# RWKV-7 recurrence in a decoder trunk: decay applied after the state's addition, norms folded, gate applied last

## The chip, the cores and the metric

One core of one Trainium2 chip runs the whole program. The metric is device time in microseconds (us); a kernel is run several times and the median counts. The engines of the core are named as in the profile: PE (TensorE, matrix products), PEld (its weight loads), DVE (VectorE), ACT (ScalarE), POOL (GpSimd) and SP (SyncE, which issues the transfers). Each engine works through its own instructions in a fixed order and waits on semaphores for the others.

## What is computed

Two decoder layers for one sequence of 256 tokens of width 2048, in fp32: an RWKV-7 time mixing layer and a differential attention layer, each followed by a gated MLP. The change touches only the time mixing. Its core, per head of 64:

```python
kk = kk / jnp.maximum(jnp.sqrt(jnp.sum(kk * kk, -1, keepdims=True)), 1e-12)
k = k * (1 + (a - 1) * k_a)
decay = jnp.exp(-jnp.exp(w.astype(jnp.float32)))
# S_t = S_{t-1} (diag(w_t) + a_t^T b_t) + v_t^T k_t ;  y_t = S_t r_t
y = wkv7_scan(r_h, decay, k_h, v_h, -kk, kk * a_h)
mean = y.mean(-1, keepdims=True)
var = jnp.square(y - mean).mean(-1, keepdims=True)
y = ((y - mean) * lax.rsqrt(var + GN_EPS)).reshape(B, T, D) * lnx_g + lnx_b
bonus = jnp.sum(r_h * k_h * r_k, -1, keepdims=True) * v_h
return ((y + bonus) * g) @ w_o
```

## The kernel before

Every dense product takes fp32 weights, which come from memory in blocks of 128x512 (`raw`), are rounded by ACT to a high part (`hi`, L217), and split by DVE into a rest (`lo`, L220); PE then does three products with them (L230 to L235). So each block needs one ACT and one DVE instruction ahead of PE. There are 4 raw blocks, 5 of `hi` and 5 of `lo` in the recurrence's stage.

The recurrence is cut into 8 groups of four heads (`NG`), each of 256 tokens in 4 chunks of 64 (`NC`). `pipeline` (L1039) runs stages of different groups side by side: while `chain` and `outputs` work on group i, `lanes` works on i+1, `factors`, `corners` and `bonus` on i+2, and `products`, the dense products for k and r, on i+3. `_together` interleaves their steps by fixed paces (the table `PACE`). The framework then puts the instructions of each engine into one order; what a row waits for goes by semaphores. `issue_after` pins some products of PE behind others.

What the stages do, with the lines that matter:

- `factors` (L1116): the squared norm of k·k_k by a product with block ones (L1138), its lower bound (L1139), the sums of the log decay within a chunk (`L`, a scan, L1146), the same sums without the token's own term (`Lx`, L1148), the inverse square root of the norm (`rsqrt`, L307: logarithm, exponential, one Newton step in three DVE instructions, L313 to L315), three exponentials (L1152 to L1154), the last column of each chunk's decay (`pc`, L1155, on POOL). From these come `KB` (keys divided by the decay so far, L1170 and L1171) and `AR` (minus the unit keys times the decay before the token, L1172; r times the decay up to it, L1174). L1184 forms their products, L1187 masks them into `M`.
- `corners` (L1225): `KB` times `pc` (L1240), eight transposes into `KBT` (L1247), and a small triangular inverse on DVE (L1251 and L1253).
- `lanes` (L1264): the rest of the triangular inverse, 32x32 products.
- `chain` (L1355): per chunk, products into `b0` and `b1` (L1386, L1399), copied to `R` by ACT and DVE; a product (L1413) copied to `UV` by ACT and DVE; the product of `UV` and `KBT` (L1426) that adds to the state `S` (copy at the first chunk, L1433; decay and addition later, L1430); the outputs into `yps` (L1403, L1437). The fourth chunk updates no state.
- `outputs` (L1443): the gate's small product (`lora`), y times gain and gate (L1455), sums of squares (L1459) into the bank `us`, their scaling (L1461), the inverse square root, and the sum with the gated bonus (L1466).
- `gates` (L1343): the small products for decay and a, with weights `l2` cast at L854, and their sigmoids (L1351), which need another function table on ACT than the rest (ACT_TABLE_LOAD at L1351 and L186).

The helper `copy` records at L1090 for every engine. Banks named `pss` are two, shared by `factors`, `corners`, `bonus` and `lanes`; `psd` holds the dense products.

Of the kernel before, what the change touches and what calls it, by code (L numbers as in the profile page):

```python
# [980 lines left out]
def _fl(t):  # L981
    return t.rearrange("p j t -> p (j t)")


# [4 lines left out]
class Groups:
# [126 lines left out]
    def factors(self, g):  # L1116
# [22 lines left out]
        nc.vector.tensor_scalar(out=_fl(t1), in0=ps, scalar1=1e-24, scalar2=None, op0=ALU.max)  # L1139
# [3 lines left out]
        Lx = g1.tile([P, GT, T], F32, name="Lx")  # L1143
        eL = g1.tile([P, GT, T], F32, name="eL")
# [9 lines left out]
        nc.scalar.activation(out=Lx, in_=Lx, func=AF.Exp, scale=-KAPPA)  # L1154
        nc.gpsimd.tensor_copy(out=pc.rearrange("p j c o -> p (j c) o"), in_=_ch(_fl(eL))[:, :, C - 1:C])  # L1155
# [7 lines left out]
        nc.vector.tensor_tensor(out=a, in0=kk, in1=a, op=ALU.mult)  # L1163
# [4 lines left out]
        for par in range(2):  # L1168
# [3 lines left out]
        nc.vector.scalar_tensor_tensor(out=AR[:, :, 0, :], in0=c3, scalar=-1.0, in1=_ch(_fl(Lx)), op0=ALU.mult,  # L1172
                                       op1=ALU.mult)
        nc.vector.tensor_tensor(out=AR[:, :, 1, :], in0=_ch(_fl(r)), in1=_ch(_fl(eL)), op=ALU.mult)  # L1174
# [50 lines left out]
    def corners(self, g):  # L1225
# [3 lines left out]
        d1, d2, KB, pc = s["d1"], self.d2, s["KB"], s["pc"]  # L1229
# [10 lines left out]
        nc.vector.tensor_tensor(out=KB.rearrange("p c a s -> p c (a s)"), in0=KB.rearrange("p c a s -> p c (a s)"),  # L1240
                                in1=pc.rearrange("p j c o -> p (j c) o").broadcast_to([P, GT * NC, 2 * C]),
                                op=ALU.mult)
        yield
# [111 lines left out]
    def chain(self, g):  # L1355
# [36 lines left out]
        for c in range(NC):  # L1392
# [30 lines left out]
            if c < NC - 1:  # L1423
                for jj in range(GT):
                    for h in range(2):
                        mm = nc.tensor.matmul(sp[rows[h], jj, :], lhsT=KBT[:, jj * NC + c, h * 64:h * 64 + 64],  # L1426
                                              rhs=UV[:, jj, c, h, :], start=True, stop=True)
                if c:
                    for jj in range(GT):
                        nc.vector.scalar_tensor_tensor(out=Sn[:, jj, :], in0=S[:, jj, :], scalar=pc[:, jj, c, :],  # L1430
                                                       in1=sp[:, jj, :], op0=ALU.mult, op1=ALU.add)
                else:
                    nc.vector.tensor_copy(out=Sn, in_=sp)  # L1433
# [9 lines left out]
    def outputs(self, g):  # L1443
# [8 lines left out]
        yield from t.lora(self.lp, self.mids, g, 2, lambda ps: self.copy(PACE["eg"], _fl(rs), ps))  # L1452
        nc.scalar.activation(out=y2, in_=yps, func=AF.Square)
        for jj in range(GT):
            nc.vector.scalar_tensor_tensor(out=y[:, jj, :], in0=yps[:, jj, :], scalar=t.p("lnx_g", j0 + jj),  # L1455
                                           in1=rs[:, jj, :], op0=ALU.mult, op1=ALU.mult)
# [85 lines left out]
```

## Time and profile before

| | us |
|---|---|
| median of three runs | 2493.4 |
| lowest, highest | 2493.0, 2501.9 |
| the profiled execution, as timed | 2495.5 |
| its span in the trace | 2493.2 |

The profile's rows are of that one execution. The recurrence's groups take from about 140 to about 580 us of the span; ahead of them lie the token shift and the products for v and the small products, behind them the output product, the attention and the MLPs. How to read the rows: a busy time says how long an engine worked; a wait is the idle time of an engine just before an instruction, put down to the instruction that ended last of those that it needed. In rows of the timeline the first number is the start, the second the duration, and brackets hold the idle time before it. "x16" counts instructions.

### The profile page before, as it was taken

Reading aid. Unit: us, or ns where it says so; the run is one execution under the profiler, and the core shown is the slowest. Engines: PE = TensorE matmul, PEld = TensorE weight load, DVE = VectorE, ACT = ScalarE, POOL = GpSimd, SP = SyncE. Lnnn points to the kernel's source line nnn. Section 1 sums busy time; section 2 is a strip of 40 time slices with the busy share of each in tenths; the row PEclk is TensorE's granted clock in tenths of the full one; section 3 lists DMA queues with packets and bytes.
Section 4 is the critical chain, followed back from the end, with each engine's and each line's share of the span. In section 5 each row is a group of like instructions: output and inputs, shape, how many; then the busy total and the mean of one; then the engine's idle time right before and its main releaser. Section 6 shows DMA issues by size and latency. Waiting matters only on the chain.

```text
span 2493.2 us, 53177 instructions
## 1 busy us (share of the span) xinstructions
PE 2430.3 (97%) x18618; PEld 2160.0 (87%) x18618; DVE 1902.1 (76%) x4282; ACT 1497.6 (60%) x3415; POOL 155.1 (6%) x200
## 2 busy tenths in 40 slices
PE   8999999998999999999999999999999999999997
PEld 7988888777988888888889999988988888888886
DVE  8978888878987777776666866778987777776665
ACT  7755565546766666665555766666766666655554
POOL 0020000002100000001111000003100000001111
PEclk9999999999999999999999999999999999999999
DMA  7644443444566666667665555556566666666663
GB/s 242 192 125 114 116 108 100 115 128 148 162 200 190 190 189 189 190 190 226 189 187 162 174 173 167 175 174 184 167 197 188 187 188 187 189 187 186 190 188 122
DMA packets 276717, 428.49 MB, mean 172 GB/s; under 512 B 60632, under 2 KB 83168, under 8 KB 276448
## 3 DMA queue, kind: packets, MB, share of 16 engines
q1 hardware_dynamic: 276448, 425.10, 58.9%
q8 instruction: 145, 2.38, 0.4%
q14 instruction: 124, 1.02, 0.1%
HBM read 420.25 MB, written 6.31 MB: 171 GB/s over the span
## 4 chain that ended last, share of the span: by engine, by line
PE 82%; DVE 10%; DMA 3%; issue 2%; ACT 2%; SPq 0%; POOL 0%; ACTq 0%; DVEq 0%; POOLq 0%
PE psd L234 43%; PE psd L235 22%; DVE lo L220 3%; PE psd L230 2%; PE psd L232 2%; PE psd L231 2%; DMA raw<-in_rkv 2%; PE psd L283 1%; PE psd L285 1%; PE psd L284 1%; ACT hi L217 1%; PE lnst L339 1%; PE psd L926 1%; PE psd L925 0%; PE psd L927 0%
## 5 line engine op out<-in xcount | busy, mean ns | idle before, releaser
L217 ACT CAST hi<-raw 128x256 fp32r<-128x256 f32 (+3 forms) x2236 | 1078.1, 489 | 805.3 <-PE psd L234 555.9
L220 DVE TENSOR_TENSOR lo<-raw,hi 128x256 fp32r<-128x256 f32 (+3 forms) x2236 | 1148.6, 539 | 483.5 <-ACT hi L217 379.3
L234 PE MATMUL psd<-S,hi 128*128 128x512 f32 x2976 | 1044.1, 395 | 1.2 <-ACT hi L217 0.7
L235 PE MATMUL psd<-S,lo 128*128 128x256 f32 x2976 | 833.5, 280 | 0.5 <-DVE lo L220 0.4
L234 PEld LDWEIGHTS psd<-S,hi 128*128 128x128 f32 x2976 | 559.6, 188 | 131.2 <-ACT hi L217 1.8
L235 PEld LDWEIGHTS psd<-S,lo 128*128 128x128 f32 x2976 | 559.2, 188 | 2.0 <-DVE lo L220 1.9
L234 PE MATMUL psd<-hs,hi 128*128 128x512 f32 x1290 | 451.5, 394 | 0.0
L235 PE MATMUL psd<-hs,lo 128*128 128x256 f32 x1290 | 361.0, 280 | 0.0
L234 PEld LDWEIGHTS psd<-hs,hi 128*128 128x128 f32 x1290 | 241.8, 187 | 56.2 <-ACT hi L217 0.6
L235 PEld LDWEIGHTS psd<-hs,lo 128*128 128x128 f32 x1290 | 243.1, 188 | 0.1
L230 PE MATMUL psd<-S,hi 128*128 128x256 f32 x512 | 149.9, 293 | 9.0 <-ACT hi L217 9.0
L232 PE MATMUL psd<-S,lo 128*128 128x256 f32 x512 | 147.3, 288 | 3.7 <-DVE lo L220 3.6
L231 PE MATMUL psd<-S,hi 128*128 128x256 f32 x512 | 145.5, 284 | 0.0
L234 PE MATMUL psd<-S1r,hi 128*128 128x512 f32 x276 | 106.8, 419 | 3.3 <-ACT hi L217 2.0
L230 PEld LDWEIGHTS psd<-S,hi 128*128 128x128 f32 x512 | 98.1, 192 | 13.0 <-ACT hi L217 9.0
L232 PEld LDWEIGHTS psd<-S,lo 128*128 128x128 f32 x512 | 98.0, 191 | 6.4 <-DVE lo L220 5.2
L231 PEld LDWEIGHTS psd<-S,hi 128*128 128x128 f32 x512 | 98.3, 192 | 0.7 <-issue 0.6
L230 PE MATMUL psd<-S1r,hi 128*128 128x256 f32 x284 | 85.5, 301 | 0.0
L539 DVE SCALAR_TENSOR_TENSOR gc<-gp,cpar,gc 128x256 f32<-128x256 f32 x172 | 82.9, 482 | 2.6
L234 PE MATMUL psd<-S1a,hi 128*128 128x512 f32 x240 | 84.4, 395 | 0.0
L232 PE MATMUL psd<-S1r,lo 128*128 128x256 f32 x284 | 80.8, 284 | 0.3 <-DVE lo L220 0.3
L231 PE MATMUL psd<-S1r,hi 128*128 128x256 f32 x284 | 81.0, 285 | 0.0
(298 smaller groups left out, 3414.7 us busy)
## 6 DMA issues: line engine op xcount, KB each, us to landing
raw<-in_ff_up SPq DMA_DIRECT2D x676, 256.0 KB, 3.7
raw<-in_ff_down SPq DMA_DIRECT2D x320, 256.0 KB, 2.9
raw<-in_rkv SPq DMA_DIRECT2D x192, 256.0 KB, 3.8
raw<-in_da_qk SPq DMA_DIRECT2D x122, 256.0 KB, 3.6
raw<-in_da_v SPq DMA_DIRECT2D x64, 256.0 KB, 3.2
raw<-in_da_o SPq DMA_DIRECT2D x64, 256.0 KB, 3.8
raw<-in_rw_o SPq DMA_DIRECT2D x50, 256.0 KB, 3.5
raw<-in_ff_down SPq DMA_DIRECT2D x32, 192.0 KB, 2.4
```

Of the source, the lines that this page charges most:

```text
L217: nc.scalar.copy(out=hi[:, :s * P], in_=r)
L220: eng.tensor_tensor(out=lo[:, :s * P], in0=r, in1=hi[:, :s * P].bitcast(F32), op=ALU.subtract)
L230: nc.tensor.matmul(ps[:, :T], lhsT=hi, rhs=xs[:, :T], start=first, stop=False)
L231: nc.tensor.matmul(ps[:, :T], lhsT=hi, rhs=xs[:, T:], start=False, stop=False)
L232: nc.tensor.matmul(ps[:, :T], lhsT=lo, rhs=xs[:, :T], start=False, stop=last)
L234: nc.tensor.matmul(ps, lhsT=hi, rhs=xs, start=first, stop=False)
L235: nc.tensor.matmul(ps[:, T:], lhsT=lo, rhs=xs[:, :T], start=False, stop=last)
L283: nc.tensor.matmul(o, lhsT=xh, rhs=hi, start=k == 0 and b == 0, stop=False)
L284: nc.tensor.matmul(o, lhsT=xh, rhs=lo, start=False, stop=False)
L285: nc.tensor.matmul(o, lhsT=xl, rhs=hi, start=False, stop=k == KT - 1 and b == T // P - 1)
L339: self.nc.tensor.matmul(st, lhsT=self.c("onesd"), rhs=t, start=not self.ln_open and n == 0, stop=stop and n == 1)
L539: nc.vector.scalar_tensor_tensor(out=gc, in0=g[:, k:k + T], scalar=cw(k, j), in1=gc, op0=ALU.mult, op1=ALU.add)
```

## The change

- The decay of a chunk (`pc`) is no longer multiplied into `KB`. In its place the updated state is multiplied: S becomes (S + update) times `pc`, in two instructions over both tiles of the group (L1437 and L1438 of the changed kernel), and one at the first chunk.
- The exponentials of the decay go into a tile `eL` with a column of ones ahead of each chunk. The decay before a token is then the same tile read one column back, so `Lx` and its exponential go. The exponentials no longer wait for the inverse square root, which used `eL` as scratch.
- The minus sign moves from `AR` to the product of the unit keys and a.
- A new function `rsqrt_neg` gives minus the inverse square root: ACT squares the first estimate with the scale folded in, and DVE does the Newton step in two instructions. It reads its input with scale and addition folded in, so the outputs' scaling goes, and it may read PSUM. The lower bound of the keys' norm becomes a Relu on ACT.
- In `outputs`, ACT multiplies y by the gain, the gate is kept in the tile `Lx`, and gate times (bonus minus y) comes last, since y carries the minus sign. The sums of squares go to a `pss` bank, held until the Newton step has read it.

```diff
+    def rsqrt_neg(self, v, e, l, scale, bias, add):
+        nc.scalar.activation(out=l, in_=v, func=AF.Ln, scale=scale, bias=bias)
+        nc.scalar.activation(out=e, in_=l, func=AF.Exp, scale=-0.5)
+        nc.scalar.activation(out=l, in_=e, func=AF.Square, scale=math.sqrt(0.5 * scale))
+        nc.vector.scalar_tensor_tensor(out=l, in0=v, scalar=add, in1=l, op0=ALU.add, op1=ALU.mult)
+        nc.vector.scalar_tensor_tensor(out=e, in0=l, scalar=-1.5, in1=e, op0=ALU.add, op1=ALU.mult)
...
-        nc.vector.tensor_scalar(out=_fl(t1), in0=ps, scalar1=1e-24, scalar2=None, op0=ALU.max)
+        nc.scalar.activation(out=_fl(t1), in_=ps, func=AF.Relu, bias=self.eps[:, 0:1])
...
-        nc.vector.tensor_tensor(out=Lx, in0=L, in1=sw, op=ALU.subtract)
-        t.rsqrt(_fl(t1), _fl(kk), GT * T, _fl(eL))
-        nc.scalar.activation(out=eL, in_=L, func=AF.Exp, scale=-KAPPA)
+        nc.scalar.activation(out=eL[:, :, 1:], in_=_ch(_fl(L)), func=AF.Exp, scale=-KAPPA)
         nc.scalar.activation(out=en, in_=L, func=AF.Exp, scale=KAPPA)
-        nc.scalar.activation(out=Lx, in_=Lx, func=AF.Exp, scale=-KAPPA)
+        t.rsqrt_neg(_fl(t1), _fl(kk), _fl(L), 1.0, self.eps[:, 1:2], 1e-24)
...
-        nc.vector.tensor_tensor(out=KB.rearrange("p c a s -> p c (a s)"), in0=KB.rearrange("p c a s -> p c (a s)"),
-                                in1=pc.rearrange("p j c o -> p (j c) o").broadcast_to([P, GT * NC, 2 * C]),
-                                op=ALU.mult)
...
+                new = sp
                 if c:
-                    for jj in range(GT):
-                        nc.vector.scalar_tensor_tensor(out=Sn[:, jj, :], in0=S[:, jj, :], scalar=pc[:, jj, c, :],
-                                                       in1=sp[:, jj, :], op0=ALU.mult, op1=ALU.add)
-                else:
-                    nc.vector.tensor_copy(out=Sn, in_=sp)
+                    new = Sn
+                    nc.vector.tensor_tensor(out=Sn, in0=S, in1=sp, op=ALU.add)
+                nc.vector.tensor_tensor(out=Sn, in0=new, in1=pc[:, :, c, :].broadcast_to([P, GT, C]), op=ALU.mult)
...
-            nc.vector.scalar_tensor_tensor(out=y[:, jj, :], in0=yps[:, jj, :], scalar=t.p("lnx_g", j0 + jj),
-                                           in1=rs[:, jj, :], op0=ALU.mult, op1=ALU.mult)
+            nc.scalar.mul(y[:, jj, :], yps[:, jj, :], t.p("lnx_g", j0 + jj))
...
-        nc.vector.tensor_tensor(out=bon, in0=bon, in1=rs, op=ALU.mult)
-        nc.vector.tensor_scalar(out=_fl(y2), in0=ps, scalar1=1.0 / 64, scalar2=GN_EPS, op0=ALU.mult, op1=ALU.add)
-        t.rsqrt(_fl(y2), _fl(rs), GT * T, _fl(g1.tile([P, GT, T], F32, name="Lx")))
+        t.rsqrt_neg(ps, _fl(rs), _fl(y2), 1.0 / 64, self.eps[:, 2:3], 64 * GN_EPS)
         nc.vector.tensor_tensor(out=y, in0=y, in1=rs, op=ALU.mult)
-        nc.vector.tensor_tensor(out=self.V[:, j0:j0 + GT, :], in0=y, in1=bon, op=ALU.add)
+        nc.vector.tensor_tensor(out=y, in0=bon, in1=y, op=ALU.subtract)
+        nc.vector.tensor_tensor(out=self.V[:, j0:j0 + GT, :], in0=y, in1=gate, op=ALU.mult)
```

The orders of the engines shift with it. PE's order stays the same to within a few dense products; three places on DVE and ACT follow. Rows of the changed kernel carry its own line numbers: L1104 is the helper `copy`, L863 the cast of `l2`, L1357 and L1225 are L1351 and L1215, L1218 and L1150 are L1208 and L1136, L1322 is the transpose L1316, L1171 and L1169 are L1160 and L1158.

The first place is on DVE, in the middle of the pipeline: the copy of `UV` at a chain's first chunk, and the first state `S`. Before:

```order
L1090 COPY UV<-us 64x128
L315 SCALAR_TENSOR_TENSOR kk<-eL,kk 128x512
L1160 TENSOR_SCALAR t_5538<-wa,par 128x256
L1158 SCALAR_TENSOR_TENSOR kk<-k,par,kk 128x256
L1433 COPY S_2099<-us 128x128
L1158 SCALAR_TENSOR_TENSOR kk<-k,par,kk 128x256
```

Changed:

```order
L220 TENSOR_TENSOR lo<-raw,hi 128x512 x2
L1104 COPY UV<-us 64x128
L220 TENSOR_TENSOR lo<-raw,hi 128x512
L313 SCALAR_TENSOR_TENSOR L<-t_5516,L 128x512
L1438 TENSOR_TENSOR S_2099<-us,pc 128x128
L314 SCALAR_TENSOR_TENSOR kk<-L,kk 128x512
```

The state's first instruction stood behind steps after the Newton step; now it stands right behind the Newton step's first instruction and a split of weights.

The second place is the third chunk's copy of `UV`, on ACT and on DVE. ACT before:

```order
L1090 COPY R<-b_4812 128x64
L1208 ACTIVATE r<-r,par 128x256
L217 CAST hi<-raw 128x512
L1208 ACTIVATE r<-r,par 128x256
L217 CAST hi<-raw 128x512
L1090 COPY W_4575<-pss 128x8x16
L1136 ACTIVATE t_5538<-k,par 128x256
L1090 COPY UV<-us 64x128
```

ACT changed:

```order
L1104 COPY R<-b_4796 128x64
L217 CAST hi<-raw 128x512
L1218 ACTIVATE r<-r,par 128x256
L1104 COPY W_4561<-pss 128x8x16
L1104 COPY UV<-us 64x128
L1104 COPY M<-W_4561 32x8x32 x2
L1218 ACTIVATE r<-r,par 128x256
L1150 ACTIVATE t_5516<-k,par 128x256 x2
```

DVE before:

```order
L220 TENSOR_TENSOR lo<-raw,hi 128x512
L1090 COPY k<-psd 128x512
L220 TENSOR_TENSOR lo<-raw,hi 128x512
L1316 STREAM_TRANSPOSE T_5990<-W_5346 128x256
L1090 COPY UV<-us 64x128
```

DVE changed:

```order
L1104 COPY k<-psd 128x512
L220 TENSOR_TENSOR lo<-raw,hi 128x512
L1104 COPY UV<-us 64x128
L1322 STREAM_TRANSPOSE T_5964<-W_5326 128x256
L1104 COPY M<-W_5326 32x8x32 x2
```

On both engines the copy of `UV` now comes ahead of work that stood before it: the square of k and one scaling of r on ACT, the transpose on DVE.

The third place is on ACT, from the outputs' logarithm to the first copies of `UV` of the next chain. Before:

```order
L311 ACTIVATE Lx<-o_y_4581 128x512
L217 CAST hi<-raw 128x512
L312 ACTIVATE o_rs<-Lx 128x512
L854 CAST l_4729<-l2r 128x256
L1351 ACT_TABLE_LOAD
L1351 ACTIVATE wa<-psd,par 128x256 x4
L186 ACT_TABLE_LOAD
L1215 ACTIVATE bon<-bon,par 128x256 x2
L1090 COPY UV<-us 64x2x128
L311 ACTIVATE eL<-t_4767 128x512
L217 CAST hi<-raw 128x512
L1090 COPY UV<-us 64x2x128
```

Changed:

```order
L310 ACTIVATE o_y_4572<-pss,eps 128x512
L311 ACTIVATE o_rs<-o_y_4572 128x512
L312 ACTIVATE o_y_4572<-o_rs 128x512
L217 CAST hi<-raw 128x512 x2
L863 CAST l_4713<-l2r 128x256
L1357 ACT_TABLE_LOAD
L1357 ACTIVATE wa<-psd,par 128x256 x2
L1104 COPY UV<-us 64x2x128
L1357 ACTIVATE wa<-psd,par 128x256 x2
L186 ACT_TABLE_LOAD
L1225 ACTIVATE bon<-bon,par 128x256 x2
L1104 COPY UV<-us 64x2x128
```

The logarithm reads the bank itself; a square and a second cast come in ahead of the cast of `l2`; the first copy of `UV` goes between the sigmoids, and the second one stands directly behind the bias of the bonus.

More of the change, by code (lines that the diff above doesn't have):

```diff
@@ L1019, in open @@
         nc.gpsimd.memset(self.UV, 0.0)
+        self.eL = fx.tile([P, GT * NC, C + 1], F32, name="eL")
+        nc.gpsimd.memset(self.eL[:, :, 0:1], 1.0)
+        self.eps = fx.tile([P, 3], F32, name="eps")
+        for n, e in enumerate((-1e-24, 1e-24, GN_EPS)):
+            nc.gpsimd.memset(self.eps[:, n:n + 1], e)
         self.Z = fx.tile([P, 8, 32], F32, name="Z")
@@ L1147, in factors @@
                                          op0=ALU.mult, op1=ALU.add)
-        nc.vector.tensor_tensor(out=Lx, in0=L, in1=sw, op=ALU.subtract)
         en = sw
         yield
-        t.rsqrt(_fl(t1), _fl(kk), GT * T, _fl(eL))
-        nc.scalar.activation(out=eL, in_=L, func=AF.Exp, scale=-KAPPA)
+        nc.scalar.activation(out=eL[:, :, 1:], in_=_ch(_fl(L)), func=AF.Exp, scale=-KAPPA)
         nc.scalar.activation(out=en, in_=L, func=AF.Exp, scale=KAPPA)
-        nc.scalar.activation(out=Lx, in_=Lx, func=AF.Exp, scale=-KAPPA)
-        nc.gpsimd.tensor_copy(out=pc.rearrange("p j c o -> p (j c) o"), in_=_ch(_fl(eL))[:, :, C - 1:C])
+        t.rsqrt_neg(_fl(t1), _fl(kk), _fl(L), 1.0, self.eps[:, 1:2], 1e-24)
+        nc.gpsimd.tensor_copy(out=pc.rearrange("p j c o -> p (j c) o"), in_=eL[:, :, C:C + 1])
         yield
@@ L1161, in factors @@
                                     op0=ALU.subtract, op1=ALU.mult)
-        nc.vector.tensor_tensor(out=a, in0=kk, in1=a, op=ALU.mult)
+        nc.vector.scalar_tensor_tensor(out=a, in0=kk, scalar=-1.0, in1=a, op0=ALU.mult, op1=ALU.mult)
         nc.vector.scalar_tensor_tensor(out=k, in0=t1, scalar=1.0, in1=k, op0=ALU.add, op1=ALU.mult)
@@ L1171, in factors @@
             nc.vector.tensor_tensor(out=self.half(KB[:, :, 1 - par, :], par), in0=a_, in1=e_, op=ALU.mult)
-        nc.vector.scalar_tensor_tensor(out=AR[:, :, 0, :], in0=c3, scalar=-1.0, in1=_ch(_fl(Lx)), op0=ALU.mult,
-                                       op1=ALU.mult)
-        nc.vector.tensor_tensor(out=AR[:, :, 1, :], in0=_ch(_fl(r)), in1=_ch(_fl(eL)), op=ALU.mult)
+        nc.vector.tensor_tensor(out=AR[:, :, 0, :], in0=c3, in1=eL[:, :, :C], op=ALU.mult)
+        nc.vector.tensor_tensor(out=AR[:, :, 1, :], in0=_ch(_fl(r)), in1=eL[:, :, 1:], op=ALU.mult)
         yield
@@ L1228, in corners @@
         s = self.st[g]
-        d1, d2, KB, pc = s["d1"], self.d2, s["KB"], s["pc"]
+        d1, d2, KB = s["d1"], self.d2, s["KB"]
         KBT = s["KBT"] = self.g3.tile([P, GT * NC, P], F32, name="KBT")
@@ L1451, in outputs @@
         rs = g1.tile([P, GT, T], F32, name="o_rs")
-        yield from t.lora(self.lp, self.mids, g, 2, lambda ps: self.copy(PACE["eg"], _fl(rs), ps))
+        gate = g1.tile([P, GT, T], F32, name="Lx")
         nc.scalar.activation(out=y2, in_=yps, func=AF.Square)
         for jj in range(GT):
-            nc.vector.scalar_tensor_tensor(out=y[:, jj, :], in0=yps[:, jj, :], scalar=t.p("lnx_g", j0 + jj),
-                                           in1=rs[:, jj, :], op0=ALU.mult, op1=ALU.mult)
+            nc.scalar.mul(y[:, jj, :], yps[:, jj, :], t.p("lnx_g", j0 + jj))
+        yield from t.lora(self.lp, self.mids, g, 2, lambda ps: self.copy(PACE["eg"], _fl(gate), ps))
+        ps = self.pst()
+        nc.tensor.matmul(ps, lhsT=t.x("bd1"), rhs=_fl(y2), start=True, stop=True)
         yield
-        ps = self.bank("us")
-        nc.tensor.matmul(ps, lhsT=t.x("bd1"), rhs=_fl(y2), start=True, stop=True)
-        nc.vector.tensor_tensor(out=bon, in0=bon, in1=rs, op=ALU.mult)
-        nc.vector.tensor_scalar(out=_fl(y2), in0=ps, scalar1=1.0 / 64, scalar2=GN_EPS, op0=ALU.mult, op1=ALU.add)
-        yield
-        t.rsqrt(_fl(y2), _fl(rs), GT * T, _fl(g1.tile([P, GT, T], F32, name="Lx")))
+        t.rsqrt_neg(ps, _fl(rs), _fl(y2), 1.0 / 64, self.eps[:, 2:3], 64 * GN_EPS)
         yield
         nc.vector.tensor_tensor(out=y, in0=y, in1=rs, op=ALU.mult)
-        nc.vector.tensor_tensor(out=self.V[:, j0:j0 + GT, :], in0=y, in1=bon, op=ALU.add)
+        nc.vector.tensor_tensor(out=y, in0=bon, in1=y, op=ALU.subtract)
+        nc.vector.tensor_tensor(out=self.V[:, j0:j0 + GT, :], in0=y, in1=gate, op=ALU.mult)
         if g >= NG - 3:
```

5 lines of the change are left out of this document (2 added, 3 removed).

## The prediction

> **What bounds the kernel now.** First the busy table and the chain on the page.
>
> ```profile
> PE 2430.3 (97%) x18618; PEld 2160.0 (87%) x18618; DVE 1902.1 (76%) x4282; ACT 1497.6 (60%) x3415; POOL 155.1 (6%) x200
> PE 82%; DVE 10%; DMA 3%; issue 2%; ACT 2%; SPq 0%; POOL 0%; ACTq 0%; DVEq 0%; POOLq 0%
> ```
>
> The tensor engine is busy 97% of the span and makes up 82% of the chain that ends last. The change touches only the recurrence, so the second view is the table by stretches (columns: PE, PEld, DVE, ACT and POOL busy, granted clock, DMA).
>
> ```profile
> 140.00:240.00 100.00, 91.70 (x1160) 84.01 (x1158) 76.06 (x164) 54.62 (x106) 13.75 (x20) 0.97 0.46 122
> 240.00:460.00 220.00, 209.86 (x3479) 186.48 (x3480) 187.93 (x437) 126.66 (x268) 10.19 (x12) 0.99 0.42 112
> 460.00:600.00 140.00, 133.83 (x1712) 106.33 (x1710) 115.16 (x280) 71.73 (x161) 2.80 (x8) 0.98 0.45 132
> 700.00:1300.00 600.00, 600.00 (x3443) 524.87 (x3442) 431.10 (x965) 360.68 (x825) 21.17 (x24) 1.00 0.68 195
> ```
>
> From 700 on PE never idles, and nothing of the change is there. From 140 to 600 PE idles 8.3 + 10.1 + 6.2 = 24.6 us, DVE is busy 85% in the middle stretch (187.93 of 220), ACT 58%. So even with every idle stretch gone the change could win about 25 us and what the clock loses. Third view, what PE waited for from 140 to 600 (us, times, longest):
>
> ```profile
> PE us L1426 <- DVE UV L1090: 5.9, 6, 1.6
> PE us L1366 <- DVE k L1090: 2.3, 1, 2.3
> PE psd L230 <- DVE Tl L1253: 1.8, 1, 1.8
> PE psd L230 <- ACT l L854: 1.7, 4, 0.6
> PE pss L1184 <- DVE AR L1174: 1.6, 1, 1.6
> PE b L1386 <- ACT UV L1090: 1.4, 4, 0.4
> PE pss L1303 <- DVE T L1296: 1.3, 1, 1.3
> ```
>
> Most are waits for VectorE. They are small, so engine totals decide nothing here; the place of each late instruction does.
>
> ```profile
> 298.83 0.45 PE L1426 MATMUL us<-UV,KBT 128*64 128x64 f32 x8 [1.45 <-DVE UV L1090]
> 345.16 0.45 PE L1426 MATMUL us<-UV,KBT 128*64 128x64 f32 x8 [0.78 <-DVE UV L1090]
> 391.92 0.45 PE L1426 MATMUL us<-UV,KBT 128*64 128x64 f32 x8 [1.00 <-DVE UV L1090]
> 439.39 0.45 PE L1426 MATMUL us<-UV,KBT 128*64 128x64 f32 x8 [1.57 <-DVE UV L1090]
> ```
>
> One wait comes back in each group, every 46 to 47 us, at the third chunk of the state. After the last of the four the granted clock falls (next to last columns: clock, DMA share, GB/s):
>
> ```profile
> 438.00:440.00 2.00, 0.61 (x16) 0.55 (x16) 1.31 (x5) 1.93 (x7) 0.00 (x0) 1.00 0.50 156
> 440.00:442.00 2.00, 2.00 (x21) 1.86 (x18) 1.74 (x4) 1.00 (x2) 0.00 (x0) 0.71 0.15 54
> 442.00:444.00 2.00, 2.00 (x26) 1.44 (x25) 1.34 (x4) 0.21 (x1) 0.00 (x0) 0.50 0.56 196
> 444.00:446.00 2.00, 2.00 (x43) 1.96 (x44) 1.65 (x3) 0.37 (x1) 0.00 (x0) 0.94 0.48 105
> ```
>
> The loss is (0.29 + 0.50 + 0.06) x 2 = 1.7 us of work. I read it as caused by the idle 1.39 us in the row before it.
>
> **The change, part by part: work.** The prices:
>
> ```profile
> L1240 DVE TENSOR_TENSOR KB<-KB,pc 128x1024 f32<-128x1024 f32 x8 | 9.7, 1213 | 0.0
> L1455 DVE SCALAR_TENSOR_TENSOR o_y<-yps,par,o_rs 128x256 f32<-128x256 f32 x16 | 7.0, 478 | 3.4 <-ACT o_rs L1090 3.4
> L314 DVE SCALAR_TENSOR_TENSOR eL<-eL,t 128x512 f32<-128x512 f32 x8 | 5.5, 685 | 0.1
> L1430 DVE SCALAR_TENSOR_TENSOR S<-S,pc,us 128x64 f32<-128x64 f32 x32 | 7.6, 275 | 0.8 <-PE us L1426 0.6
> L1433 DVE COPY S<-us 128x128 f32<-128x128 f32 x8 | 2.2, 278 | 0.2 <-PE us L1426 0.2
> L1351 ACT ACTIVATE wa<-psd,par 128x256 f32<-128x256 f32 x32 | 12.8, 473 | 1.4 <-PE psd L232 1.3
> L1453 ACT ACTIVATE o_y<-yps 128x512 f32<-128x512 f32 x8 | 4.8, 595 | 0.6 <-PE yps L1437 0.6
> L1154 ACT ACTIVATE Lx<-Lx 128x512 f32<-128x512 f32 x8 | 5.0, 619 | 0.0
> ```
>
> VectorE loses, in each of 8 groups: the product of KB with the decay (1.213), the two gated gains (0.956), and five passes over 128x512 (the bound, Lx, a square in each of the two norms, the mean's scaling) at 0.685 = 3.4. That is 5.6 us a group, 45 in all, from 85% to about 73% of a period. The state's update stays level: three decays and two additions at the 0.278 of a 128x128 copy are 1.39 against 0.278 + 4 x 0.275 = 1.38. ScalarE gains a bound (0.595), two squares (2 x 0.62) and two gains (2 x 0.473) and loses one exponential (0.619): 2.2 us a group, 58% to about 62%. None of this is on PE. What counts is where it sits before a wait, below.
>
> **The third chunk's copy of UV (gain).**
>
> ```profile
> 343.84 0.26 ACT L1090 COPY W<-pss 128x128 f32<-128x128 f32 x1
> 344.00 0.51 ACT L1136 ACTIVATE t<-k,par 128x256 f32<-128x256 f32 x1
> 344.13 0.45 DVE L1316 STREAM_TRANSPOSE T<-W 128x256 f32<-128x256 f32 x1 [0.52 <-ACT W L1090]
> 344.53 0.26 ACT L1090 COPY UV<-us 64x128 f32<-64x128 f32 x1
> 344.83 0.28 DVE L1090 COPY UV<-us 64x128 f32<-64x128 f32 x1 [0.25 <-ACT UV L1090]
> ```
>
> ScalarE's copy stands behind a square of k (0.51), VectorE's behind a transpose that waits 0.52 for ScalarE. In the changed order both squares follow the copies, one scaling of r and one weight cast fewer stand before, and the transpose follows VectorE's copy. That is over 1 us on ScalarE and 0.97 on VectorE, against a wait of 0.78 to 1.57. I take the four waits as gone: **4.8 us**, and the clock's drop at 440 with the longest of them: **1.7 us**. Bounds: 0 to 8.
>
> By the Trainium skill, page "TensorE: Matmul & The Clock Gate", section "HAM oscillation — how this bites in real kernels", PE should stay free of idle gaps above about 3.4 us, so a gap of 1.4 us would not lower the clock. Here the drop follows such a gap directly, so by the trace the rule is too lenient; by the rule the 1.7 us stay and the sum below would be 4.2.
>
> **Outputs' norm and the gates (gain).** Ln now reads the sums in PSUM, without VectorE's scaling (0.685) between, and the matmul stands 12 products earlier; one square and one cast (about 0.6 each) come in ahead of the cast of l2. Net earlier, so I count the 1.7 us of PE waiting for that cast (l L854) as gone, bounds 0 and 1.7. The first copies of UV no longer have a logarithm and a cast between them, but PE arrives 10 products earlier: I take half of the 1.4 us at L1386, **0.7**, bounds -1 and 1.4. Together **2.4**.
>
> **The first chunk's state (loss).**
>
> ```profile
> 329.77 0.45 PE L1426 MATMUL us<-UV,KBT 128*64 128x64 f32 x8
> 330.46 0.27 DVE L1433 COPY S<-us 128x128 f32<-128x128 f32 x1
> 331.04 0.34 PE L1399 MATMUL b<-S,AR 64*64 64x64 f32 x8
> ...
> 335.18 0.45 PE L1426 MATMUL us<-UV,KBT 128*64 128x64 f32 x8
> ...
> 340.10 0.34 PE L1399 MATMUL b<-S,AR 64*64 64x64 f32 x8
> ```
>
> S is ready at 330.73 and wanted at 331.04: 0.3 us of slack. Now the decay of S (same length) stands right behind the first fused Newton step, which waits for ScalarE's square. ScalarE does UV, exponential, cast, square: from its UV copy at 328.51, 0.26 + 3 x 0.62 brings 330.6; the step (0.685) ends at 331.3, the decay at 331.6. One more product lies ahead of L1399, so PE waits about **0.5 us** in each of the six groups that run beside a later group's factors: **3.0 us**. Bounds: 0 each (the casts come early) and 1.1 (one more cast of 0.62 in between). At the second chunk an addition, a cast's remainder (0.69) and the decay take 1.2 us in place of 0.47; there 4.9 us lie between L1426 (335.18) and its L1399 (340.10), which hide it. VectorE's copy of R after the first chunk comes later too, and 12 products in place of 15 lie ahead of L1413, which needs it; I leave that at 0, bounds 0 and 0.4 us a group.
>
> **Start and end.** In group 0 the factors become longer on ScalarE (three casts now lie between bound, logarithm, exponential and square: about 2 us later), but PE has 26 more products before L1184. I leave its 1.6 us of waiting as it is, bounds -1.5 and 1.6. L1366's 2.3 us wait comes from the stage ahead and stays. The last group's chain from sums to gate has eight steps before and after: 0. Transposes of KB no longer wait for the decay, but no row shows PE waiting there: 0.
>
> **Sum.** 4.8 + 1.7 + 2.4 - 3.0 = 5.9 us gained. The profiled execution took 2495.5 us (its span 2493.2); that becomes 2489.6. The median of the runs shown is 2493.4, 2.1 lower, so the forecast is **2487.5**.
>
> **Rivals.**
> *The waits only move.* PE keeps its order to within a few products, and each copy of R and UV still waits in line on two in-order engines. For it: ScalarE has 2.2 us more a group, in the half where the first chunks run. Against: VectorE loses 5.6. Gains and losses cancel: 2493.4.
> *The drop at 440 stays,* because something else causes it. The gain is 4.2: 2489.2. This is the outcome by the rule named above.
> *Slower: the Newton step couples the state to the weights.* A cast of weights now stands between logarithm and square, and casts do wait:
>
> ```profile
> ACT hi L217 <- DMA raw<-in_rkv: 49.1, 21, 11.8
> ```
>
> That is 2.3 us a time (21 times from 140 to 600). If one falls in that place in most groups, S comes 1.1 us or more later still, PE idles 1.6 us, the length that went ahead of the drop at 440, and each time costs 1.6 + 1.7. Six times this, less the 7.2 us that would still be gained, is 12.6: 2506. It decides from a wait of about 1 us for that cast. Against it: in the group of the last timeline no cast waited between 325 and 331 us; those waits lie elsewhere.
> *Much faster: VectorE's lag goes as a whole.* Then all of L1426 (5.9), Tl (1.8), l (1.7), L1184 (1.6), L1386 (1.4) and L1303 (1.3) go, with two drops of the clock (3.4) and no new wait: 17.1, so 2476.3. Against it: four of these are chains through ScalarE or a DMA, not lag.
>
> **Numbers.** Forecast (2482 to 2491) 0.42, waits move 0.21, drop stays 0.10, slower 0.11, much faster 0.16. Faster by over 0.5% (below 2480.9; about what a measurement of this kernel can tell from no change) needs the last: 0.17 with a little of the forecast's edge. Slower by over 0.5% (above 2505.9) needs the upper half of the slow one: 0.08. Range 2475 to 2501: it leaves out half of the fast and most of the slow case.
>
> **What would show it.** L1426 waiting for UV at the third chunk under 0.3 us in the groups from 280 to 440, and the clock at 1.00 around 440: the gain. L1399 waiting for DVE S at the first chunk, with VectorE idle for ScalarE's square ahead: the loss and its size. DVE busy near 1857 us and ACT near 1515: the prices. PE's waits from 140 to 600 falling below 15 us in all would speak for the fast rival. Wrong would be: a PE wait for a bank (pss) that the outputs' sums now hold until the Newton step has read them, or new drops of the clock in every group.

## The result and the profile after

The changed kernel took 2482.9 us (median of 6 runs, 2478.7 to 2484.6); the kernel before took 2499.2 us in the runs beside it (6 runs, 2493.0 to 2502.0). The ratio is 0.9937, 95% interval 0.9920 to 0.9954: 0.63% faster, and the interval leaves out no change. The two profiled executions took 2495.5 and 2482.4 us, 13.1 apart, where 5.9 were forecast.

The page of the changed kernel, busy time and chain:

```profile
PE 2428.7 (98%) x18618; PEld 2160.7 (87%) x18618; DVE 1864.6 (75%) x4218; ACT 1514.7 (61%) x3447; POOL 143.3 (6%) x204
PE 86%; DVE 6%; ACT 3%; DMA 2%; issue 2%; SPq 0%; POOL 0%; ACTq 0%; DVEq 0%; POOLq 0%
```

The table by stretches of the changed kernel, columns as in the prediction:

```profile
140.00:240.00 100.00, 94.92 (x1291) 87.61 (x1290) 73.34 (x165) 58.97 (x113) 6.37 (x20) 1.00 0.48 133
240.00:460.00 220.00, 218.66 (x3600) 193.05 (x3598) 173.88 (x421) 147.39 (x310) 4.37 (x15) 1.00 0.40 112
460.00:600.00 140.00, 130.28 (x1518) 104.89 (x1515) 105.30 (x256) 70.60 (x161) 5.88 (x9) 0.95 0.45 134
```

The middle stretch is where the gain shows best: PE idles 1.3 us in it instead of 10.1. The stretch behind it looks worse: 9.7 us idle instead of 6.2, and a granted clock of 0.95 instead of 0.98. The changed kernel is ahead there (the product of the third chunk that started at 439.39 now starts at 425.88), so the window does not hold quite the same work; the table below goes to 700. What PE waits for longest from 140 to 600 in the changed kernel:

```profile
PE pss L1309 <- DVE T L1302: 2.4, 2, 1.6
PE lnst L348 <- DVE X L412: 1.9, 3, 0.9
PE psd L230 <- DVE Tl L1259: 1.7, 1, 1.7
PE psd L235 <- issue: 1.7, 1, 1.7
PE us L1432 <- DVE UV L1104: 1.5, 2, 1.1
PE us L1372 <- DVE k L1104: 1.4, 1, 1.4
```

The wait for UV (L1426 before, L1432 now) fell from 5.9 to 1.5 us, and 1.1 of these lie behind 460; those for AR, for l of the gates and at the first copies of UV are gone. The third chunk in the changed kernel, timeline of ScalarE, VectorE and PE (start, duration):

```profile
332.46 0.62 ACT L217 CAST hi<-raw 128x512 fp32r<-128x512 f32 x1 [1.45 <-PE psd L231]
332.98 0.51 ACT L1218 ACTIVATE r<-r,par 128x256 f32<-128x256 f32 x1
333.39 0.24 ACT L1104 COPY W<-pss 128x128 f32<-128x128 f32 x1
333.66 0.26 ACT L1104 COPY UV<-us 64x128 f32<-64x128 f32 x1
333.95 0.28 DVE L1104 COPY UV<-us 64x128 f32<-64x128 f32 x1
334.68 0.45 PE L1432 MATMUL us<-UV,KBT 128*64 128x64 f32 x8
```

UV is ready at 334.23 and PE starts on it at 334.68 without having waited. And a place where the changed kernel loses time, rows of PE and of ScalarE, and the windows there:

```profile
461.59 0.45 PE L1432 MATMUL us<-UV,KBT 128*64 128x64 f32 x8 [1.11 <-DVE UV L1104]
464.33 1.05 PE L1309 MATMUL pss<-T,M 32*32 32x16 f32 x64 [1.63 <-DVE T L1302]
460.43 0.62 ACT L217 CAST hi<-raw 128x512 fp32r<-128x512 f32 x1 [2.40 <-DMA raw<-in_rw_o]
460.95 0.25 ACT L1104 COPY UV<-us 64x128 f32<-64x128 f32 x1
```

```profile
462.00:464.00 2.00, 0.70 (x11) 0.32 (x7) 2.00 (x6) 0.00 (x0) 0.00 (x0) 0.82 0.11 35
464.00:466.00 2.00, 1.67 (x66) 1.63 (x67) 2.00 (x7) 0.00 (x0) 0.00 (x0) 0.50 0.07 16
466.00:468.00 2.00, 2.00 (x7) 1.66 (x7) 1.93 (x5) 0.00 (x0) 0.00 (x0) 0.50 0.77 188
```

Two waits stand close together, and the half clock begins within the second. The first comes from a weight cast that waits 2.40 us for its transfer ahead of the copy of UV (2.20 in the repeat, where PE then waits 0.93). So the balance of any version needs two columns: time that PE idles, and time lost to a lower clock. Both are read from windows of 2 us from 120 to 700: idle is 2.00 less PE's busy time, clock loss is 2.00 x (1 - granted clock). What lies outside this sum hardly moves: the span less the sum is 2450.1 to 2452.0 us in the four profiles of before and after (2445 to 2456 in the others, additional products left out; the clock loss counts a slower clock in full, so it is an upper estimate). That spread of 11 us means that a sum tells more about where time goes than about how much. The table gives idle plus clock loss; "first bonus" is the start of the first group's bonus matmul (line L1211 before, L1221 after), the first fixed point behind the start.

| kernel | median us | ratio (95%) | first bonus | 120-240 | 240-460 | 460-700 | sum |
|---|---|---|---|---|---|---|---|
| before | 2499.2 | 1 | 183.2 | 8.6+3.4 | 10.1+1.7 | 12.3+5.1 | 41.2 |
| before_repeat | 2496.7 (one run) | | 182.7 | 9.1+3.4 | 11.7+1.7 | 12.1+6.8 | 44.8 |
| after | 2482.9 | 0.9937 (0.9920-0.9954) | 178.2 | 5.3+0 | 1.3+0 | 14.2+8.5 | 29.3 |
| after_repeat | 2483.5 | 0.9947 (0.9931-0.9962) | 179.0 | 5.8+1.7 | 1.0+0 | 12.4+6.8 | 27.7 |
| fill_factors | 2483.3 | 0.9944 (0.9927-0.9960) | 179.7 | 5.1+1.7 | 1.7+0 | 13.6+5.1 | 27.2 |
| fill_outputs | 2487.9 | 0.9958 (0.9943-0.9973) | 179.0 | 6.1+0 | 3.8+0 | 11.6+10.2 | 31.7 |
| decay_alone | 2505.0 | 1.0035 (1.0023-1.0047) | 181.9 | 8.8+3.4 | 10.1+5.1 | 16.5+12.0 | 55.9 |
| factors_alone | 2498.0 | 1.0005 (0.9995-1.0014) | 178.0 | 5.6+1.7 | 10.3+8.5 | 11.5+6.8 | 44.4 |
| outputs_alone | 2488.5 | 0.9973 (0.9962-0.9983) | 179.5 | 8.5+1.7 | 6.5+3.4 | 12.8+3.4 | 36.3 |
| after_less_decay | 2480.2 | 0.9941 (0.9929-0.9954) | 179.4 | 7.0+0 | 2.4+0 | 11.9+3.4 | 24.7 |
| factors_warm | 2492.7 | 0.9986 (0.9975-0.9996) | 179.7 | 4.3+5.1 | 3.0+0 | 12.0+5.1 | 29.5 |
| factors_vv | 2491.6 | 0.9980 (0.9970-0.9990) | 179.4 | 3.8+5.1 | 8.3+0 | 12.7+11.9 | 41.8 |
| before_vv | 2493.5 | 0.9986 (0.9973-0.9999) | 181.9 | 8.4+5.1 | 5.5+0 | 12.4+8.5 | 39.9 |
| less_vv | 2480.5 | 0.9938 (0.9922-0.9954) | 179.5 | 5.5+3.4 | 2.1+0 | 11.3+1.7 | 24.0 |

One of the 12 executions of factors_vv took 4768.4 us; its ratio leaves that one out.

By the means of the two profiles of each, the change takes 5.9 us off the start, 11.5 off the middle, and adds 2.8 behind it: 14.5 us. The spans fall by as much (2494.1 to 2479.5). The 2.8 is not clear of the scatter: behind 460 the two repeats differ by 0.3 alone (18.9 and 19.2).

### The profile page after: what moved, and what is told of

Its sections match the earlier page's. It is cut to its first block, busy times and chain, and to the rows that moved or that the text cites. A ratio compares the mean times of both kernels' runs of the same rounds, so it can differ in the third digit from the quotient of the medians.

```text
span 2480.4 us, 53145 instructions
## 1 busy us (share of the span) xinstructions
PE 2428.7 (98%) x18618; PEld 2160.7 (87%) x18618; DVE 1864.6 (75%) x4218; ACT 1514.7 (61%) x3447; POOL 143.3 (6%) x204
## 4 chain that ended last, share of the span: by engine, by line
PE 86%; DVE 6%; ACT 3%; DMA 2%; issue 2%; SPq 0%; POOL 0%; ACTq 0%; DVEq 0%; POOLq 0%
PE psd L234 43%; PE psd L235 22%; PE psd L230 3%; PE psd L231 3%; PE psd L232 3%; DVE lo L220 2%; PE psd L283 1%; PE psd L285 1%; PE psd L284 1%; DMA raw<-in_rkv 1%; PE pss L1194 1%; ACT hi L217 1%; PE lnst L348 1%; DVE mp L808 1%; PE psd L935 1%
## 5 line engine op out<-in xcount | busy, mean ns | idle before, releaser
L220 DVE TENSOR_TENSOR lo<-raw,hi 128x256 fp32r<-128x256 f32 (+3 forms) x2236 | 1148.7, 539 | 498.4 <-ACT hi L217 391.6
L230 PE MATMUL psd<-S1r,hi 128*128 128x256 f32 x284 | 85.2, 300 | 0.0
L235 PE MATMUL psd<-S1r,lo 128*128 128x256 f32 x276 | 81.4, 295 | 1.7 <-issue 1.7
L232 PE MATMUL psd<-S1r,lo 128*128 128x256 f32 x284 | 80.8, 284 | 0.2 <-DVE lo L220 0.2
```

Of the source, the lines that this page charges most:

```text
L220: eng.tensor_tensor(out=lo[:, :s * P], in0=r, in1=hi[:, :s * P].bitcast(F32), op=ALU.subtract)
L230: nc.tensor.matmul(ps[:, :T], lhsT=hi, rhs=xs[:, :T], start=first, stop=False)
L232: nc.tensor.matmul(ps[:, :T], lhsT=lo, rhs=xs[:, :T], start=False, stop=last)
L235: nc.tensor.matmul(ps[:, T:], lhsT=lo, rhs=xs[:, :T], start=False, stop=last)
```

## Experiments

**What repeats.** Both kernels were run again unchanged.

> The kernel before, unchanged, for a second profile. If the 5.0 us that the changed kernel had gained when the bonus matmul of the first group starts (183.2 us before, 178.2 after) come from the change, this profile shows that matmul at 183.2 within 1 us, the first weight-driven wait for k near 2.3 us and half-clock windows near 150-154, 202-206 and 440-444 us. If they are differences from one execution to the next, it starts anywhere from 178 to 184 and the half-clock windows lie elsewhere or are missing.

> The changed kernel, unchanged. A gain that belongs to it: ratio 0.992 to 0.996 again, the bonus matmul of the first group at 178.2 within 1 us, period of the steady groups 45.6 us. If the start was a matter of one execution: that matmul anywhere from 178 to 184, and a ratio that may reach 0.997.

The start belongs to the change: the first bonus comes at 182.7 against 179.0, each within 1 us of the first profile. In the middle the repeats agree within 1.6 us. The half clock at 440 is in both profiles of before and in neither of after; the one near 204, gone in the first profile of after, is back in the second: that 1.7 us is not the change's.

**Work against place.** The same additional work (three sums of 128x512, 0.68 us each, in each group) at two places of the changed kernel.

```
# fill_factors: behind the bound, the scan and the Newton step
nc.vector.tensor_reduce(out=self.junk[:, :2], in_=t1, axis=AX.X, op=ALU.add)   # likewise L, kk
# fill_outputs: behind the gains (y) and, twice, behind the sums (y2)
nc.vector.tensor_reduce(out=self.junk[:, :2], in_=y, axis=AX.X, op=ALU.add)
```

> The changed kernel with three additional sums over 128x512 on VectorE in the factors of each group (about 2 us a group, results not used), at the places of the work that was removed there. They move ScalarE's square of k and VectorE's transpose ahead of the third chunk's copies of UV again. Theory of the place: four waits of PE for UV come back, 0.8 to 1.6 us each, with at least one half-clock stretch of 1.7 us: 5 to 7 us slower than the changed kernel, about 2488 to 2490 (ratio 0.996). Theory of the work: the gain goes with VectorE's work, 2.0 of 5.6 us a group given back: 2.0/5.6 x 15.7 = 5.6 us, ratio 0.996 too; the waits for UV stay away, PE's idle time grows everywhere.

> The changed kernel with three additional sums over 128x512 on VectorE in the outputs of each group (about 2 us a group, results not used). The order around the third chunk's copies of UV stays that of the changed kernel. Theory of the place: no wait for UV comes back, time within 1.5 us of the changed kernel (ratio 0.9937 within 0.0006). Theory of the work: 2.0/5.6 x 15.7 = 5.6 us slower than the changed kernel, ratio 0.996.

Both expectations failed for the first: nothing was given back (2483.3 against 2483.5), and no wait for UV came back although ScalarE's square stands ahead of the copies again. The second came out 4.4 us above after_repeat in the medians. The intervals of the two overlap, so the time alone does not separate them; the waits from 240 to 460 do. In fill_outputs a new one stands there, for the copy of r behind the additional sums:

```profile
PE psd L230 <- DVE r L1105: 3.0, 5, 1.1
```

For this run the theory of the work had named the ratio well (0.996, measured 0.9958), and the theory of the place had not (within 0.0006 of 0.9937); but the same work in the factors cost nothing. Equal work, two prices: the gain is not in proportion to VectorE's work, and neither the square nor the transpose that I had blamed brings the waits back. Both runs keep about 3.6 of the 5.6 us a group that VectorE was spared, so they do not exclude that a smaller saving is enough.

**The parts alone.** Each part of the change put into the kernel before, and the change without its decay.

```
# decay_alone: the state's edit and no product of KB with pc
nc.vector.tensor_tensor(out=Sn, in0=new, in1=pc[:, :, c, :].broadcast_to([P, GT, C]), op=ALU.mult)
# factors_alone: Relu bound, rsqrt_neg, eL one column back; outputs and decay as before
# outputs_alone: gain on ScalarE, rsqrt_neg from the bank, gate last; the rest as before
# after_less_decay: after, with KB <- KB * pc and the state's update of before
```

> The kernel before with the decay moved from KB to the updated state, and nothing else of the change. Theory of the queue (what stands ahead of the third chunk's copies on ScalarE decides, above all the weight casts and the scalings of r between the copy of R and the copy of W): here two casts, a scaling and a square still stand there as before, so PE waits for UV in the third chunk 0.8 to 1.6 us in each of four groups, the half-clock stretch at 440 stays, and the bonus matmul of the first group starts at 181 to 183: 0 to 3 us gained, ratio 0.9988 to 1.000. Theory of the work: 1.21 of 5.6 us a group of VectorE's work go, 0.22 x 14.5 = 3.2 us, ratio 0.9987.

> The kernel before with the factors' formulas of the change alone (bound, Newton step, one column back), decay and outputs as before. Theory of the queue: AR of the first group is ready earlier, so the start's 4 us (its wait of 1.6, a half-clock stretch of 1.7, part of the wait for k) come with this part: bonus matmul of the first group at 178 to 180. In the third chunk two casts and a square stay ahead of UV, but no scaling of r: waits of 0.3 to 1.0 us. Gain 5 to 8 us, ratio 0.997 to 0.998. Theory of the work: 2.06 of 5.6 us a group go, 5.3 us, ratio 0.9979, spread over all groups, the start no more than 0.7 of it.

> The kernel before with the outputs of the change alone (norm read from the bank, gate last), decay and factors as before. Theory of the queue: the four waits of PE for l of the gates (1.7) and the four for UV at L1386 (1.4) go; in the third chunk two casts and a scaling stay ahead of W but the squares stand behind UV, so the waits fall from 1.2 to about 0.7 us each; the start stays at 182 to 183. Gain 3 to 7 us, ratio 0.997 to 0.999. Theory of the work: 2.33 of 5.6 us a group go, 6.0 us, ratio 0.9976.

> The changed kernel with the decay put back on KB (product of 128x1024 on VectorE, 1.21 us a group, and the state's update as before). Theory of the queue: one cast and one square stand ahead of the third chunk's copies, no wait of over 0.5 us for UV comes back: within 2 us of the changed kernel, ratio 0.994 to 0.995, and the bonus matmul of the first group at 178 to 180. Theory of the work: 3.2 us slower than the changed kernel, ratio 0.9955.

The decay, the first edit that the change names, makes the kernel before slower (1.0035), and the changed kernel is no slower without it. Factors alone gain the start and lose it again in the middle; outputs alone gain 0.27%; the two together (after_less_decay) 0.59%. Neither theory's sum over parts would give that. For the decay alone both had expected no loss (0.9988 to 1.000, and 0.9987), for the factors alone both had expected a gain (0.997 to 0.998, and 0.9979): both failed. The two others came out within the ratios that the theory of the queue had named, though the start of outputs_alone did not stay at 182 to 183 (179.5). By the table decay_alone loses most behind 460 us (28.5 where before has 17.4 and 18.9). The stretch from 460 to 600 of decay_alone, and then of after_less_decay:

```profile
460.00:600.00 140.00, 130.20 (x1667) 102.33 (x1666) 110.77 (x271) 67.78 (x152) 2.27 (x6) 0.94 0.43 127
```

```profile
460.00:600.00 140.00, 132.31 (x1550) 107.24 (x1549) 109.79 (x265) 72.72 (x168) 8.93 (x13) 0.99 0.44 133
```

Why the factors lose in the middle is in the timeline of factors_alone at the third chunk (ScalarE, then VectorE and PE):

```profile
387.76 0.62 ACT L217 CAST hi<-raw 128x512 fp32r<-128x512 f32 x1 [1.98 <-DMA raw<-in_rkv]
388.28 0.26 ACT L1104 COPY W<-pss 128x128 f32<-128x128 f32 x1
388.44 0.51 ACT L1150 ACTIVATE t<-k,par 128x256 f32<-128x256 f32 x1
388.97 0.26 ACT L1104 COPY UV<-us 64x128 f32<-64x128 f32 x1
389.36 0.28 DVE L1104 COPY UV<-us 64x128 f32<-64x128 f32 x1
389.70 0.50 PE L1436 MATMUL us<-UV,KBT 128*64 128x64 f32 x8 [2.44 <-DVE UV L1104]
```

A weight cast ahead of the copies of W and UV waits 1.98 us for its DMA, and holds everything behind it on ScalarE, VectorE's transpose of W too. The square of k stands between the copies as well, but in fill_factors it does so without any wait. The same pattern, smaller, is in the kernel before at 437: two casts with 1.00 and 0.36 of waiting ahead of that copy of W. Each of its three other groups has such a wait too (1.37; 0.34 and 0.25; 0.49).

```profile
436.15 0.62 ACT L217 CAST hi<-raw 128x512 fp32r<-128x512 f32 x1 [1.00 <-DMA raw<-in_rkv]
437.55 0.62 ACT L217 CAST hi<-raw 128x512 fp32r<-128x512 f32 x1 [0.36 <-DMA raw<-in_rkv]
```

In the changed kernel one cast stands there, and in none of the four groups does it wait for a DMA (332.46 above). From 240 to 460 the casts of the kernel before wait like this:

```profile
ACT hi L217 <- DMA raw<-in_rkv: 16.8, 9, 6.7
```

The changed kernel has none of it (1.5 us in the repeat), its two fills, after_less_decay and less_vv 0 to 3.2, and all other profiles 10.4 to 34.1. So I changed the theory: not the sum of VectorE's work, nor the square, but whether a cast that waits for weights stands ahead of the copies; the half clock then follows from PE's idle time.

Why the weights come late can be seen one step further back. In the kernel before, ahead of the casts from 434 to 437.55 (VectorE, then the issues of SyncE):

```profile
429.95 0.68 DVE L220 TENSOR_TENSOR lo<-raw,hi 128x512 fp32r<-128x512 f32 x1
430.78 1.89 DVE L220 TENSOR_TENSOR lo<-raw,hi 128x512 fp32r<-128x512 f32 x3
430.70 2.81 SPq L211 DMA_DIRECT2D raw<-in_rkv  x4
```

A transfer into a block of `raw` has to wait until VectorE's split has read that block (from 240 to 460 SyncE waits 104.6 us for L220 ahead of these issues, 46 times). VectorE works without a pause from 426 to 435.5, its splits of earlier blocks come only at 429.95 to 432.7, and the four transfers go out right behind them. So the late cast goes back to splits that stand late in VectorE's queue. No run moves the splits alone, so how far VectorE's lag is behind the casts' waits stays open: a threshold in VectorE's saving, somewhere between the 2.3 us a group that the outputs spare alone and the 3.6 that both fills keep, would fit the runs as well.

**Is it the idle time that halves the clock?** Products that nobody wants, where PE idled.

```
# factors_warm: ahead of the third chunk's state products, groups 1 to 4
for _ in range(6):
    nc.tensor.matmul(rb[0][:, 2 * C:2 * C + T], lhsT=t.x("bd1"), rhs=t.x("reset", T), start=False, stop=False)
```

> The factors' formulas alone (the run factors_alone) with six products of 128x256 more on the tensor engine, wanted by nobody, just ahead of the third chunk's state products in groups 1 to 4: about 1.8 us of work where PE waited 1.67 to 2.44 us for UV. Theory that the half clock follows from PE's own idle time: the four half-clock stretches at 290, 342, 390 and 438 us (8.5 us lost between 240 and 460) go, the products fill time that was idle: 6 to 9 us faster than factors_alone, about 2490, ratio 0.997. Theory that the clock falls for another reason: the stretches stay, and what the products outlast of the waits comes on top: 0 to 2 us slower, ratio 1.0005 to 1.001.

The windows around the fourth of these places, of factors_alone and then of factors_warm:

```profile
436.00:438.00 2.00, 0.33 (x6) 0.28 (x6) 1.30 (x4) 1.94 (x6) 0.00 (x0) 0.94 0.75 192
438.00:440.00 2.00, 2.00 (x21) 1.80 (x19) 1.68 (x4) 0.60 (x2) 0.00 (x0) 0.50 0.15 44
440.00:442.00 2.00, 2.00 (x31) 1.74 (x31) 0.88 (x2) 1.43 (x3) 0.00 (x0) 0.71 0.35 114
```

```profile
434.00:436.00 2.00, 2.00 (x22) 1.52 (x22) 1.46 (x5) 1.93 (x7) 0.00 (x0) 1.00 0.56 174
436.00:438.00 2.00, 2.00 (x22) 1.79 (x20) 1.51 (x4) 1.27 (x4) 0.00 (x0) 1.00 0.19 58
438.00:440.00 2.00, 1.81 (x35) 1.42 (x35) 1.39 (x4) 0.79 (x3) 0.00 (x0) 1.00 0.34 104
```

All four half-clock stretches between 240 and 460 are gone, and the kernel is 5.3 us faster with more work on its fullest engine. It falls short of the 6 to 9 expected mostly because the six products of a group took 2.86 us, not 1.8, where the waits had been 1.67 to 2.44. The order on ScalarE up to the copies is that of factors_alone, so it is the idle time that brings the half clock.

**Is it the cast?** The copies of W and of the third chunk's UV on VectorE, past ScalarE's queue, in three kernels.

```
-            self.copy("AV"[jj], UV[r, jj, c, :, :], up[r])
+            self.copy("VV"[jj] if c == 2 else "AV"[jj], UV[r, jj, c, :, :], up[r])
-  ez='VA'
+  ez='VV'
```

> The factors' formulas alone, with the third chunk's two copies of UV and the copy of W before it on VectorE, so that the second weight cast on ScalarE (which waits up to 2 us for the weights' DMA) no longer stands ahead of them. Theory of the queue (the cast that waits for its DMA ahead of the copies makes PE wait, and those waits bring the half clock): waits for UV in the third chunk under 0.5 us each, no half-clock stretch between 240 and 460, 12 to 16 us faster than factors_alone, 2482 to 2486, ratio 0.994 to 0.9955, without the outputs' and the decay's part of the change. Theory of the work on VectorE (which gets 0.5 us a group more): no gain over factors_alone, ratio 1.000 to 1.001.

> The kernel before with the same two edits. Here VectorE's remainder of the second cast still stands ahead of the copies of W and UV, so the cast that waits for its DMA is still ahead of them, by way of VectorE. Theory of the queue: waits for UV of 0.8 us and more stay in the third chunk, the start is unchanged: ratio 0.999 to 1.001. If it is ScalarE's square and its scaling of r that make the copies late: the four waits (4.8 us) and the half clock at 440 (1.7 us) go, ratio 0.9975.

> The changed kernel with the decay back on KB and the third chunk's copies of UV and W on VectorE: a version that may beat both. Theory of the queue: there was no wait to win between 240 and 460 (2.4 us of idle time in all), so only the wait at 461 (0.6) can go, and with it perhaps the half clock at 464 to 468 (1.7): 0 to 2 us faster than after_less_decay, ratio 0.993 to 0.9945. Theory of the work: VectorE gets 0.5 us a group more, 1 to 2 us slower, ratio 0.9945 to 0.995.

With factors alone the waits for UV fall from 7.6 us (four, up to 2.4) to 3.3 (four, up to 0.9), every half clock between 240 and 460 goes, and 6.4 us are gained, against the 12 to 16 expected: the first cast still holds VectorE's remainder and its copy of k ahead of them, PE waits 3.0 us for M now (0.6 at a time), and the half clock from 460 to 700 grew from 6.8 to 11.9 us. In the kernel before my expectation was wrong: only one wait for UV of 0.7 us is left of 5.9. I had taken VectorE's remainder ahead of the copies for that of the last cast; it belongs to the cast before, and the last one had been passed by. So the edit supports the cast as the cause, but not against ScalarE's square, which it passes too; the square alone is excluded by fill_factors. It gives VectorE more work, and the waits for UV shrink all the same, while the casts still wait for their weights (31.2 us in before_vv, 10.5 in factors_vv): what counts for PE is the place of the copies. The time followed only to 0.9986: by the table the middle gains 7.1 us on the mean of before, 460 to 700 gives back 2.8 and the start 1.3. less_vv is not to be told from the change or from the change without its decay; no version here is shown to beat the changed kernel.

## Why the prediction was right, and where its sum was not

The forecast of 2487.5 had the sign and its range (2475 to 2501) held 2482.9, but the gain is more than double: 13.1 us between the profiled executions and 16.4 between the medians, where 5.9 were forecast. By the ratio the outcome lies beyond the bound of 0.5%, in the corner that I gave 0.17. That the time itself falls into the band of the forecast (2482 to 2491) is luck in part: the kernel before came out at 2499.2 in the runs beside it, 5.8 above the 2493.4 that I counted from. In the middle stretch nearly all that the rival "VectorE's lag goes" names went; whether by way of that lag stays open, since the late casts go back to VectorE's splits. Of the signs that I named, the third chunk's waits and the clock at 440 came as forecast and the first chunk's wait did not; PE idles 16.1 us from 140 to 600, just above the 15 that would have spoken for that rival. Term by term:

- **Work.** Forecast 1857 us on VectorE and 1515 on ScalarE; measured 1864.6 and 1514.7. Close (37.5 us spared on VectorE, 45 priced); in the middle stretch VectorE is busy 79% of the time, not 73%, and ScalarE 67%, not 62%.
- **Third chunk, 4.8 us, and the clock at 440, 1.7 us.** Right: 0.4 us of waiting for UV is left from 240 to 460 (0.2 in the repeat), no half clock. My reason was half right: of the items that I listed ahead of the copies, the weight cast counted, and that by its wait for weights, which I had put into a rival alone; square and transpose did not (fill_factors).
- **Outputs' norm and gates, 2.4 us.** Under-sized: 1.7 and 1.4 us went as a whole, where I had counted half of the second, and 1.0 us for lo, which I had not listed. outputs_alone gains 0.27% by itself.
- **First chunk's state, a loss of 3.0 us.** This step failed. The Newton step does stand ahead of the decay, but it was on time; no wait of PE for S of 0.2 us or more is left in either profile of the changed kernel from 240 to 460. In one group:

```profile
317.73 0.26 ACT L1104 COPY UV<-us 64x128 f32<-64x128 f32 x1
318.01 0.63 ACT L311 ACTIVATE kk<-L 128x512 f32<-128x512 f32 x1
318.55 0.60 ACT L217 CAST hi<-raw 128x512 fp32r<-128x512 f32 x1
319.06 0.63 ACT L312 ACTIVATE L<-kk 128x512 f32<-128x512 f32 x1
319.25 0.45 PE L1432 MATMUL us<-UV,KBT 128*64 128x64 f32 x8
319.80 0.68 DVE L313 SCALAR_TENSOR_TENSOR L<-t,L 128x512 f32<-128x512 f32 x1
320.40 0.28 DVE L1438 TENSOR_TENSOR S<-us,pc 128x128 f32<-128x128 f32 x1
320.84 0.34 PE L1405 MATMUL b<-S,AR 64*64 64x64 f32 x8
```

I let the square end 0.83 us after the start of L1432 (330.6 against 329.77); it ended after 0.44. ScalarE's three steps do follow its copy of UV (317.73), as I had lined them up, but their rows overlap, so that they took 1.96 us from that copy's start and not 2.12, and L1432 itself starts 1.52 us behind that copy, not 1.26. S is ready 1.43 us after L1432 starts, not 1.83, and wanted after 1.59, where it was 1.27 before: no wait. The one product more on PE, which I had counted as next to nothing, is that 0.32.
- **Start, 0.** Failed: 5.9 us by the means. AR's wait of 1.6 us is gone wherever the factors' formulas are in (no such wait in factors_alone, the changed kernel or its fills; 1.5 and 1.6 in decay_alone and outputs_alone); part of it comes back as a longer wait for M (1.1 and 1.5, where it was 0.4). The rest is less wait for k (2.3 and 2.9 before, 1.4 and 1.6 after) and half clocks; in the other kernels that wait is 1.3 to 2.2 without pattern, so how much of it is the change's stays open.
- **End, 0.** Not settled: 2.8 us lost from 460 to 700 by the means, 0.3 between the repeats. New in both profiles of the changed kernel is the wait for UV at 461 (1.1 and 0.9), behind the cast that waits for its transfer. Without the decay's move that wait is 0.6 and the clock loss there 3.4 us in place of 8.5 and 6.8; why the last groups react so is open.

The rival that the drop at 440 stays did not come about, and factors_warm shows idle time as the cause of such drops. The slower rival had the right mechanism, a cast that waits for its weights ahead of something PE needs; it sat at the third chunk, not at the first, and in the changed kernel the cast that stands there no longer waits for weights. factors_alone is what it looks like when it does.

## What to carry to other kernels

Price an edit by what stands behind it in the queue, not by what it removes: here the edit with the largest saving on one instruction (1.2 us a group) gained nothing, and the larger part of the gain came where a weight cast no longer stood, waiting for its DMA, ahead of two short copies. When a transfer is late, ask who freed its buffer: here it was another engine's queue. Where the fullest engine idles more than a microsecond at a time, look at the granted clock behind each wait, and count idle time and clock loss together; parts of a change need not add up. And when a scheduler orders the queues, an edit in one step moves casts in another: read the order around the tightest copies first.

## What the runs showed of the hardware

How long PE may idle before the clock halves. Between 240 and 460 us the 14 profiles have 48 waits of PE of 0.5 us or more. Of the 35 up to 1.25 us none was followed by half the clock; of the 13 from 1.28 to 2.44 us nine were, all three above 2 us among them, and four from 1.45 to 1.86 us were not. Seven of the nine half-clock stretches lasted 3.41 us, that is 1.7 us of work lost at 0.50; one lasted twice that (factors_alone) and one three times (decay_alone). By the Trainium skill, page "TensorE: Matmul & The Clock Gate", section "HAM oscillation — how this bites in real kernels", gaps above about 3.4 us are the ones to avoid. The traces do not bear that out as the gap that is safe: here 1.28 us was enough.

Where a wait falls matters beside its length. In each of the 14 profiles, from 100 us on and up to the last stretch of the execution, the half clock begins and ends on one raster, that is, on points evenly spaced by 3.413 us (in the kernel before at 150.71, 201.91 and 440.84, which are 15 and 70 steps apart). Three of the four waits that were not followed (1.45, 1.70 and 1.86 us) lie across a point of that raster, with 1.35 us at most on one side; the fourth (1.62) does not, so the raster is not the whole rule.

Products that nobody wants paid for themselves: 11.4 us of them (4 groups x 2.86) in factors_warm took the place of 7.6 us of waiting and 8.5 us of lost clock.
